# A decoder step on one core: features as rows at both ends, and a norm as one product with a constant matrix

## The chip, the cores and the metric

One core of a Trainium2 chip runs the kernel, in one launch. The metric is the device time of an execution in microseconds (us). TensorE is called PE, VectorE DVE, ScalarE ACT, GpSimd POOL and SyncE SP; ACT, POOL and SP also issue DMAs, POOL those with gathered rows.

## The reference

One layer of a decoder over 256 prompt tokens and 8 x 4 sample tokens, 288 columns in all, with 2048 features, all in fp32:

```
h = h + 1/2 * SwiGLU(RMSNorm(h))                      ffn1: 2048 -> 5632 -> 2048
z = RMSNorm(h) @ w_in                                 3 x 1024 conv, 3 x 1024 q k v, 8 gate logits
h = h + [RMSNorm(conv) | RMSNorm(attention)] @ w_out
h = h + 1/2 * SwiGLU(RMSNorm(h))                      ffn2
h = h + sigmoid(RMSNorm(h) @ w_ple_gate) * (p @ w_ple_proj)
y = RMSNorm(h)
```

RMSNorm(x) is x * rsqrt(mean(x * x) + 1e-6) * gain. The sample tokens attend to 1024 past keys each: `cache_k` holds 80 pages of 128 rows (8 heads x 128 features), and `page_table` names 8 pages for each of the 8 sequences, so 64 pages of 512 KB are read. Besides y, the outputs are the new k, v, forget logits and last conv inputs.

## The kernel before

The residual lies in SBUF with features as rows, `h[128, 16, 288]` (16 tiles of 128 features, 288 tokens as columns). A weight product is made of three: weights and activations are split into a high and a low part (`whi` on ACT, line 257; `wlo` on DVE, line 258; `xh`, `xl`, lines 200 and 201), and lines 290 to 292 add hi*hi, hi*lo and lo*hi in one PSUM bank. `pair()` makes 256 output columns, in chunks of four feature tiles: 24 products of 288 columns, 3.2 us on PE. `run_steps()` goes through a list `steps` of chunks in program order; `load_upto()` issues weight loads eight ahead on SP (line 234), `split_upto()` splits five half-chunks ahead, and `defer(fn, n)` puts a piece of work n chunks later, run by `run_deferred()` in the middle of a chunk. Within one engine instructions run in order; a scheduler fixes that order when the program is built.

The stages follow each other: ffn1, the mixer (gate logits, q, k, conv, v), `w_out`, ffn2, the per-layer embedding (`ple_pair`), `finish`.

**Norms.** `squares()` adds the squared tiles into `acc[128, 288]`. `inv_rms()` (lines 168 to 181) takes three products with a column of 1/2048 that sum over the partitions, tokens as rows, then square root (ACT), reciprocal and a Newton step (DVE) on `[128, 3]`. `spread()` (lines 191 to 197), deferred, brings the 288 factors back to all partitions: three products of a diagonal with ones, and a copy to `rs`. The products run on without waiting, since `rs` is first applied to their results (line 352 and the like). There are seven norms; the one in `finish` needs no spread, since y is there with tokens as rows.

**Key cache.** `k_turn()` (lines 444 to 453) runs between the steps of ffn1, once for each of 64 pages: a gather `kg` on POOL (line 441), 32 x 32 transpositions on DVE (line 450), four DMAs on POOL to a scratch `KD` in HBM (line 452). In the mixer, 32 units `k_scores(n)`, two pages each, read `KT` (1 MB, three buffers), which SP loads from `KD` (line 239); each unit is 16 products (line 704, `KSTEP` sets one every 1.5 chunks).

**Outputs.** `natural()` (lines 623 to 629) transposes three blocks on PE and copies them on DVE, to write tokens as rows: for 8 key heads (`k_out`), 8 value heads and 16 y tiles (`yt`, line 1070 on). `conv_out` (line 882 on) transposes eight tiles, and lines 567 and 569 the forget logits.

**Ends.** Line 466 runs a square root on a `[128, 1]` tile at the start, which brings an ACT table load there. Line 1062 does the same while the last pair runs.

Of the kernel before, what the change touches and what calls it, by code (L numbers as in the profile page):

```python
# [25 lines left out]
P = 128  # L26
# [3 lines left out]
DB = 8  # L30
# [19 lines left out]
TSTEP = 16  # L50
# [8 lines left out]
def constants():  # L59
# [15 lines left out]
    put("ones", np.ones((P, NT)))  # L75
    put("meancol", np.full((P, 1), 1.0 / D))
# [16 lines left out]
def build(nc, tc, ctx, A, O):  # L93
# [69 lines left out]
    ones = const("ones")  # L163
    diag = cst.tile([P, NT], F32, name="diag")
    n0, n1, n2 = (cst.tile([P, 3], F32, name=f"n{i}") for i in range(3))
    v.memset(n0, 1.0)

    def inv_rms(squares, width):

        m = ktbank()  # L170
        for j in range(2):
            pe.matmul(m[:, j:j + 1], squares[:, j * P:j * P + P], const("meancol"), start=True, stop=True)
        pe.matmul(m[:NS, 2:3], squares[:, SEQ:], const("meancol"), start=True, stop=True)
        v.tensor_scalar(n0[:, 0:2], m[:, 0:2], float(D // width), EPS, ALU.mult, ALU.add)
        v.tensor_scalar(n0[:NS, 2:3], m[:NS, 2:3], float(D // width), EPS, ALU.mult, ALU.add)
        s.activation(n1, n0, AF.Sqrt)
        v.reciprocal(n2, n1)
        v.scalar_tensor_tensor(n1, n2, -0.5, n0, ALU.mult, ALU.mult)
        v.tensor_tensor(n1, n1, n2, ALU.mult)
        v.scalar_tensor_tensor(n2, n1, 1.5, n2, ALU.add, ALU.mult)  # L180
        return n2

    def norm_scale(out, squares, width, chunks, more=2):

        def sums():
            r = inv_rms(squares, width)
            defer(lambda: spread(out, r), more)

        defer(sums, chunks)

    def spread(out, r):
# [37 lines left out]
    def load_upto(n):  # L229
        while state["loaded"] < min(n, len(items)):  # L230
# [180 lines left out]
    def first(c):  # L411
        run = steps[2 + c][1]

        def fn():
# [13 lines left out]
            if c == 7:  # L428
                norm_scale(rs, acc, D, 2, 1)
# [5 lines left out]
    KD = drp.tile([DB * PAGES // 2, P, 2, 4, NH * 32], F32, name="KD")  # L435

    KG = {}

    def k_fetch(j):
        KG[j] = W["kg"][0].tile([P, NH * P], F32, name="kg", tag="kg", bufs=4)  # L440
        g.indirect_dma_start(out=KG[j], out_offset=None, in_=A["cache_k"],  # L441
                             in_offset=bass.IndirectOffsetOnAxis(ap=idx[:, j:j + 1], axis=0))

    def k_turn(j):

        for i in range(3) if j == 0 else (j + 2,):
            if i < DB * PAGES:
                k_fetch(i)
        t = W["kg"][0].tile([P, 4, NH, 32], F32, name="kt", tag="kt", bufs=3)
        v.transpose(t, KG.pop(j).rearrange("p (h d c) -> p d h c", d=4, c=32))  # L450
        for i in range(4):
            g.dma_start(KD[j // 2, :, j % 2, i].rearrange("(d c) n -> c d n", c=32),  # L452
# [703 lines left out]
```

## Time and profile before

| | us |
|---|---|
| median of 3 runs | 2376.87 |
| the runs | 2375.11, 2376.87, 2378.67 |
| the profiled execution | 2380.13 |
| its span in the trace | 2378.2 |

| engine | busy us | share of the span | instructions |
|---|---|---|---|
| PE | 2350.4 | 99% | 17792 |
| DVE | 1426.0 | 60% | 2575 |
| ACT | 1052.7 | 44% | 1858 |
| POOL | 495.6 | 21% | 681 |

Products on PE are pipelined: one of 288 columns is listed with some 0.29 us, but its successor starts 0.133 us later at full clock. So the time that an instruction takes from PE is read from the starts of its neighbours, not from its duration.

### The profile page before, as it was taken

The page shows a single profiled execution, that of the slowest core. Times are in us where ns is not written, and L with a number is a line of the kernel's source. Part 1 is how long each engine was busy: PE and PEld are TensorE (multiplying, and loading weights), DVE is VectorE, ACT ScalarE, POOL GpSimd, SP SyncE. Part 2 cuts the span into 40 slices and gives each one's busy share as a digit, 9 for nine tenths or more (in the row PEclk, how much of TensorE's full clock was granted, in tenths as well). Part 3 has the DMA queues.
Part 4 walks back from the last instruction along what each step waited for, and adds up shares of the span by engine and source line. Part 5 has one row for each costly group of instructions (what it writes and reads, how often), then busy time and mean ns, then how long its engine had stood idle before and what let it go on. Part 6 is the DMA issues. An engine that isn't in the chain of part 4 may idle for free.

```text
span 2378.2 us, 45847 instructions
## 1 busy us (share of the span) xinstructions
PE 2350.4 (99%) x17792; PEld 2284.3 (96%) x17792; DVE 1426.0 (60%) x2575; ACT 1052.7 (44%) x1858; POOL 495.6 (21%) x681
## 2 busy tenths in 40 slices
PE   8999999999999999999999999999999999999997
PEld 8999999999999999888788999999999999999997
DVE  6567666666655675456456775555555555555765
ACT  6434444444444553243234454444444444444654
POOL 1044443543400121113446210000000000000110
PEclk9999999999999999999999999999999999999998
DMA  8589898898865566997887654545555555555552
GB/s 263 160 266 316 275 299 289 294 321 270 285 213 161 167 170 218 312 305 234 305 274 271 214 166 150 182 149 180 165 164 168 162 167 163 165 165 164 160 160 80
DMA packets 408601, 510.81 MB, mean 215 GB/s; under 512 B 22064, under 2 KB 376592, under 8 KB 404256
## 3 DMA queue, kind: packets, MB, share of 16 engines
q1 hardware_dynamic: 374560, 401.45, 54.1%
q0 software_dynamic: 33632, 106.13, 12.9%
q8 instruction: 139, 2.28, 0.4%
q14 instruction: 78, 0.64, 0.1%
q10 hardware_dynamic: 192, 0.32, 0.1%
HBM read 469.19 MB, written 38.63 MB: 214 GB/s over the span
## 4 chain that ended last, share of the span: by engine, by line
PE 94%; DMA 3%; issue 1%; DVE 1%; POOL 1%; ACT 0%; SPq 0%; POOLq 0%; DVEq 0%; ACTq 0%
PE mm L290 30%; PE mm L292 29%; PE mm L291 29%; PE va L704 1%; DMA page<-in_cache_v_dram,idx 1%; PE va L761 1%; PE va L290 1%; PE va L292 1%; PE va L291 1%; DMA kg<-in_cache_k_dram,idx 1%; DMA wraw<-in_w_in_dram 1%; DMA wraw<-in_w_out_dram 0%; DVE wlo L258 0%; POOL page L242 0%; PE kt L196 0%
## 5 line engine op out<-in xcount | busy, mean ns | idle before, releaser
L258 DVE TENSOR_TENSOR wlo<-wraw,whi 128x512 fp32r<-128x512 f32 x1384 | 968.7, 706 | 726.9 <-ACT whi L257 680.4
L257 ACT ACTIVATE whi<-wraw 128x512 fp32r<-128x512 f32 x1384 | 862.6, 630 | 982.4 <-PE mm L291 912.5
L290 PE MATMUL mm<-xh,whi 128*128 128x288 f32 x3680 | 1098.4, 298 | 0.2 <-DVE tg L352 0.2
L292 PE MATMUL mm<-xh,wlo 128*128 128x288 f32 x3680 | 1082.6, 294 | 3.5 <-DVE wlo L258 3.5
L291 PE MATMUL mm<-xl,whi 128*128 128x288 f32 x3680 | 1086.0, 295 | 0.0
L290 PEld LDWEIGHTS mm<-xh,whi 128*128 128x128 f32 x3680 | 690.1, 188 | 22.6 <-ACT whi L257 13.6
L292 PEld LDWEIGHTS mm<-xh,wlo 128*128 128x128 f32 x3680 | 693.2, 188 | 4.2 <-DVE wlo L258 4.2
L291 PEld LDWEIGHTS mm<-xl,whi 128*128 128x128 f32 x3680 | 691.4, 188 | 0.2
L290 PE MATMUL mm<-hh,whi 128*128 128x288 f32 x1408 | 416.8, 296 | 0.0
L291 PE MATMUL mm<-hl,whi 128*128 128x288 f32 x1408 | 415.4, 295 | 0.0
L292 PE MATMUL mm<-hh,wlo 128*128 128x288 f32 x1408 | 414.0, 294 | 0.0
L356 POOL TENSOR_TENSOR sr<-sg,rs 128x288 f32<-128x288 f32 x88 | 73.9, 840 | 1108.1 <-ACT sg L354 1108.0
L292 PEld LDWEIGHTS mm<-hh,wlo 128*128 128x128 f32 x1408 | 265.2, 188 | 0.0
L291 PEld LDWEIGHTS mm<-hl,whi 128*128 128x128 f32 x1408 | 264.4, 188 | 0.0
L290 PEld LDWEIGHTS mm<-hh,whi 128*128 128x128 f32 x1408 | 263.8, 187 | 0.0
L452 POOL DMA_DIRECT2D KD<-kt x256 | 142.4, 562 | 84.0 <-DVE kt L450 58.8
L220 POOL TENSOR_TENSOR acc<-acc,sq 128x288 f32<-128x288 f32 x60 | 50.5, 841 | 270.5 <-ACT sq L219 236.7
L450 DVE STREAM_TRANSPOSE kt<-kg 128x1024 f32<-128x1024 f32 x64 | 79.2, 1238 | 34.1 <-DMA kg<-in_cache_k_dram,idx 26.6
L376 DVE SCALAR_TENSOR_TENSOR h<-mm,h 128x288 f32<-128x288 f32 x192 | 86.9, 455 | 21.2 <-PE mm L292 20.7
L441 POOL DMA_INDIRECT kg<-in_cache_k_dram,idx x64 | 71.8, 1122 | 73.7 <-DVE idx L157 53.4
L363 ACT ACTIVATE hh<-hd 128x288 fp32r<-128x288 f32 x88 | 39.1, 445 | 99.6 <-DVE hd L361 99.4
L354 ACT ACTIVATE sg<-tg 128x288 f32<-128x288 f32 x88 | 39.1, 444 | 97.0 <-DVE tg L352 96.9
(274 smaller groups left out, 1559.0 us busy)
## 6 DMA issues: line engine op xcount, KB each, us to landing
wraw<-in_w_ffn_gate_dram SPq DMA_DIRECT2D x176, 512.0 KB, 3.9
wraw<-in_w_ffn_up_dram SPq DMA_DIRECT2D x176, 512.0 KB, 3.6
wraw<-in_w_ffn_down_dram SPq DMA_DIRECT2D x160, 512.0 KB, 3.7
wraw<-in_w_in_dram SPq DMA_DIRECT2D x96, 512.0 KB, 4.8
KD<-kt POOLq DMA_DIRECT2D x256, 128.0 KB, 5.7
KT<-KD SPq DMA_DIRECT2D x32, 1024.0 KB, 7.4
wraw<-in_w_out_dram SPq DMA_DIRECT2D x32, 512.0 KB, 4.5
wraw<-in_w_ple_gate_dram SPq DMA_DIRECT2D x32, 512.0 KB, 4.2
```

Source lines behind the costliest of these rows:

```text
L220: (v if k >= KT - last_on_v else g).tensor_tensor(acc, acc, sq, ALU.add)
L257: s.activation(hi, x, AF.Copy)
L258: v.tensor_tensor(lo, x, hi.bitcast(F32), ALU.subtract)
L290: pe.matmul(o, hi[:, j % 2, w], xh, start=f, stop=False)
L291: pe.matmul(o, hi[:, j % 2, w], xl, start=False, stop=False)
L292: pe.matmul(o, lo[:, j % 2, w], xh, start=False, stop=l)
L354: s.activation(u, t, AF.Silu)
L356: g.tensor_tensor(r, u, rs, ALU.mult)
L376: v.scalar_tensor_tensor(h[:, k, :], o, 0.5, h[:, k, :], ALU.mult, ALU.add)
L441: g.indirect_dma_start(out=KG[j], out_offset=None, in_=A["cache_k"], in_offset=bass.IndirectOffsetOnAxis(ap=idx[:, j:j + 1], axis=0))
L450: v.transpose(t, KG.pop(j).rearrange("p (h d c) -> p d h c", d=4, c=32))
L452: g.dma_start(KD[j // 2, :, j % 2, i].rearrange("(d c) n -> c d n", c=32), t[32 * i:32 * i + 32].rearrange("c d h r -> c d (h r)"))
```

## The change

**Norms.** `mean` is a 128 x 128 matrix of 1/2048. One fp32 product with it sums over the partitions and has the result on all of them, 288 columns wide; ACT takes the logarithm and exp(-ln/2), DVE makes the Newton step on `[128, 288]` in three operations. `spread`, `diag` and the square root go. The last two tiles' squares are not added in `finish` but are parts of the same product.

**Key cache.** The host hands `cache_k` over with features as rows, (page, feature) by (head, row). `KT` is filled by two gathers on POOL a unit. `k_turn`, `KD`, `kg` and the loads on SP go.

**Outputs.** k, y, the conv inputs and the forget logits are written with features as rows and are turned on the host; v stays. `finish` scales `h` in place with seven DVE and two POOL operations and writes eight pieces, alternately from SP and ACT.

**Ends.** The square root at the start goes. The table for the last norm is loaded while the last pair runs.

```diff
-    ones = const("ones")
-    diag = cst.tile([P, NT], F32, name="diag")
...
+    ones = const("ones").to_broadcast([P, NT])
...
-    def inv_rms(squares, width):
-
-        m = ktbank()
-        for j in range(2):
-            pe.matmul(m[:, j:j + 1], squares[:, j * P:j * P + P], const("meancol"), start=True, stop=True)
-        pe.matmul(m[:NS, 2:3], squares[:, SEQ:], const("meancol"), start=True, stop=True)
...
+    def log_tables():
+        tc.keep_in_program_order(s.preload_act_table_set("natural_log_exp_and_others"))
+
+    def inv_rms(out, parts, width, load=True):
+
         b = ktbank()
-        for j, n in enumerate((P, P, NS)):
-            c = slice(j * P, j * P + n)
-            v.tensor_scalar(diag[:n, c], ident[:n, :n], r[:n, j:j + 1], None, ALU.mult)
-            pe.matmul(b[:, c], ones[:n, :P], diag[:n, c], start=True, stop=True)
-        v.tensor_copy(out, b[:, :NT])
+        m = b[:, :NT]
+        for i, x in enumerate(parts):
+            pe.matmul(m, const("mean"), x, start=i == 0, stop=i == len(parts) - 1)
+        if load:
+            log_tables()
+        c = float(D // width)
+        s.activation(ra, m, AF.Ln, bias=eps, scale=c)
+        s.activation(out, ra, AF.Exp, scale=-0.5)
+        v.scalar_tensor_tensor(ra, out, -0.5 * c, out, ALU.mult, ALU.mult)
+        v.scalar_tensor_tensor(ra, m, EPS / c, ra, ALU.add, ALU.mult)
+        v.scalar_tensor_tensor(out, ra, 1.5, out, ALU.add, ALU.mult)
+
+    def norm_scale(out, squares, width, chunks):
+
+        defer(lambda: inv_rms(out, [squares], width), chunks)
...
-                t = W["kt"][0].tile([P, 2, 4, NH, 32], F32, name="KT", tag="KT", bufs=3)
-                sy.dma_start(t.rearrange("p a i h r -> p (a i h r)"), it["src"])
+                t = W["kt"][0].tile([P, 2, NH, P], F32, name="KT", tag="KT", bufs=3)
+                for i, r in enumerate(it["rows"]):
+                    g.indirect_dma_start(out=t[:, i].rearrange("p h s -> p (h s)"), out_offset=None, in_=it["src"],
+                                         in_offset=bass.IndirectOffsetOnAxis(ap=r, axis=0))
...
-    steps.insert(50 + TSTEP * 13, ([], lambda: (closed("kg"), opened("kt", "right"))))
-    for j in reversed(range(DB * PAGES)):
-        steps.insert(50 + TSTEP * j // 5, ([], lambda j=j: k_turn(j)))
-    steps.insert(46, ([], lambda: opened("kg", "right")))
-
-    warm = cst.tile([P, 1], F32, name="warm")
-    v.memset(warm, 1.0)
-    s.activation(warm, warm, AF.Sqrt)
+    steps.insert(200, ([], lambda: opened("kt", "right")))
...
+        g.dma_start(O["logfT"], lf)
...
-            pe.transpose(np_[:, j * NH:j * NH + NH], lf[:, j * P:j * P + P], ident[:NH, :NH])
...
+                if scale is None:
+                    g.dma_start(O["kT"][hh], t)
...
+            if i8 == CB - 1:
+                g.dma_start(O["convT"], M["uc"])
...
-    for i in range(4):
-        at(4 * i + 4, lambda i=i: defer(lambda: k_out(2 * i)), lambda i=i: defer(lambda: k_out(2 * i + 1), 3))
...
-                tc.keep_in_program_order(s.activation(warm, warm, AF.Sqrt))
+                log_tables()
...
-            c = slice(k * P, k * P + P)
-            defer(lambda: natural(E["yn"][:, :, c], E["ys"][:, c], y), 2)
+                E["sq", k] = w.tile([P, NT], F32, name=f"sq{k}")
+                s.activation(E["sq", k], h[:, k, :], AF.Square)
+            if k < KT - 2:
+                s.activation(h[:, k, :], h[:, k, :], AF.Copy, scale=gain("norm_final", k))
...
+        inv_rms(rs, [acc, E["sq", KT - 2], E["sq", KT - 1]], D, False)
+        for i, e in enumerate((v, g, v, v, v, g, v, v)):
+            c = slice(2 * i, 2 * i + 2)
+            if i == KT // 2 - 1:
+                for k in (KT - 2, KT - 1):
+                    v.scalar_tensor_tensor(h[:, k], h[:, k], gain("norm_final", k), rs, ALU.mult, ALU.mult)
             else:
+                e.tensor_tensor(h[:, c], h[:, c], rs.unsqueeze(1).to_broadcast([P, 2, NT]), ALU.mult)
+            (sy, s)[i % 2].dma_start(O["yT"][:, c], h[:, c])
```

Three places in the order of instructions show what moved. First, ACT at the start of the program (x is loaded to `h`, the gains to `gT`; DMAHW semaphores are those of the loads). Before:

```order
L467 DMA gT<-in_gains_dram 128x120
L466 ACT_TABLE_LOAD
L466 ACTIVATE warm<-warm 128x1 [waits DVE_49]
L200 ACTIVATE xh<-h,gT 128x288 [waits DMAHW1_49,DMAHW0_49]
L200 ACTIVATE xh<-h,gT 128x288
L257 ACTIVATE whi<-wraw 128x512 [waits DMAHW2_49]
```

and of the change:

```order
L433 DMA gT<-in_gains_dram 128x120
L190 ACT_TABLE_LOAD [waits DMAHW1_49]
L190 ACTIVATE xh<-h,gT 128x288 [waits DMAHW0_49]
L190 ACTIVATE xh<-h,gT 128x288
L249 ACTIVATE whi<-wraw 128x512 [waits DMAHW2_49]
```

The table load, which waited for nothing, now waits for the first load of x.

Second, DVE in ffn1 where the key pages begin (`idx` are the page rows, `wlo` the low halves of weights, `tg` an eviction). Before:

```order
L157 TENSOR_SCALAR idx<-ptb,consts 128x64 [waits DMAHW3_49]
L258 TENSOR_TENSOR wlo<-wraw,whi 128x512 [waits PE_49,Activation_49]
L258 TENSOR_TENSOR wlo<-wraw,whi 128x512 [waits DMAHW2_49,PE_49,Activation_49]
L450 STREAM_TRANSPOSE kt<-kg 128x1024 [waits DMASW1_49]
L258 TENSOR_TENSOR wlo<-wraw,whi 128x512 [waits PE_49,Activation_49] x2
L450 STREAM_TRANSPOSE kt<-kg 128x1024 [waits DMASW2_49]
```

and of the change:

```order
L156 TENSOR_SCALAR idx<-ptb,consts 128x64 [waits DMAHW3_49]
L250 TENSOR_TENSOR wlo<-wraw,whi 128x512 [waits PE_49,Activation_49]
L250 TENSOR_TENSOR wlo<-wraw,whi 128x512 [waits DMAHW2_49,PE_49,Activation_49]
L250 TENSOR_TENSOR wlo<-wraw,whi 128x512 [waits PE_49,Activation_49] x3
L250 TENSOR_TENSOR wlo<-wraw,whi 128x512 [waits DMAHW4_49,PE_49,Activation_49]
L344 TENSOR_TENSOR tg<-mm,rs 128x288 [waits PE_49]
```

The weight halves no longer stand behind transpositions that wait for gathers (DMASW). On POOL, the gathers of the first three units stand at this place.

Third, POOL among the key-score units of the change (`tB`, `tC` and `acc_82` belong to the conv group; before, POOL had no key loads here):

```order
L850 TENSOR_TENSOR tB<-tB,cy 128x256 [waits DVE_49]
L853 TENSOR_TENSOR tB<-tB,cy 128x32
L230 DMA KT<-in_cache_k_dram,idx 128x1024 [waits DMASW1_49,DMASW0_49,PE_49]
L850 TENSOR_TENSOR tB<-tB,cy 128x256 [waits DVE_49]
L853 TENSOR_TENSOR tB<-tB,cy 128x32
L230 DMA KT<-in_cache_k_dram,idx 128x1024
L861 TENSOR_TENSOR acc_82<-acc_82,sq 128x288 [waits Activation_49]
L230 DMA KT<-in_cache_k_dram,idx 128x1024 [waits DMASW3_49,DMASW2_49,PE_49]
```

The gathers of a unit wait for PE's products of the unit three before it, and the conv group's additions stand between them.

## Rows read from the trace of the kernel before

**Rows 1.** The profile page: its head, and the first line of its section on the chain of work that ended last (share of the span by engine).

```profile
span 2378.2 us, 45847 instructions
...
PE 94%; DMA 3%; issue 1%; DVE 1%; POOL 1%; ACT 0%; SPq 0%; POOLq 0%; DVEq 0%; ACTq 0%
```

**Rows 2.** The table of stretches, for 1400 to 2250 us. [...]

```profile
1400.00:2250.00 850.00, 850.00 (x6378) 849.78 (x6377) 474.47 (x795) 383.53 (x656) 47.52 (x58) 1.00 0.54 165
```

**Rows 3.** The timeline of PE around the norm ahead of ffn1: the last weight product before and the first after the sums of squares (lines 172 and 173), then the same for the spread (line 196). Columns here and below: start in us, duration in us, engine, line, operation, out<-in, stationary size, tile, count.

```profile
39.30 0.30 PE L292 MATMUL mm<-xh,wlo 128*128 128x288 f32 x1
...
40.02 0.40 PE L290 MATMUL mm<-xh,whi 128*128 128x288 f32 x1
...
43.18 0.29 PE L292 MATMUL mm<-xh,wlo 128*128 128x288 f32 x1
...
44.18 0.40 PE L290 MATMUL mm<-xh,whi 128*128 128x288 f32 x1
```

**Rows 4.** The timeline of PE around the score products of one prompt head (lines 805 and 806, fp32).

```profile
1222.40 0.29 PE L292 MATMUL mm<-xh,wlo 128*128 128x288 f32 x1
1222.53 0.38 PE L805 MATMUL kt<-k,q 128*128 128x128 f32 x2
1222.75 0.60 PE L806 MATMUL kt<-k,q 128*128 128x256 f32 x2
1223.00 0.48 PE L290 MATMUL mm<-xh,whi 128*128 128x288 f32 x1
```

**Rows 5.** The timeline of PE: the weight products on both sides of one key head's three transpositions (lines 625 to 627), and on both sides of the six of two y tiles.

```profile
939.53 0.29 PE L292 MATMUL mm<-xh,wlo 128*128 128x288 f32 x1
...
939.91 0.38 PE L290 MATMUL mm<-xh,whi 128*128 128x288 f32 x1
...
2275.64 0.29 PE L292 MATMUL mm<-xh,wlo 128*128 128x288 f32 x1
...
2276.35 0.38 PE L290 MATMUL mm<-xh,whi 128*128 128x288 f32 x1
```

**Rows 6.** The timelines of DVE and then of PE around the first key transpositions (line 450). In brackets stands the idle time just before an instruction and what ended it.

```profile
130.35 0.26 DVE L157 TENSOR_SCALAR idx<-ptb,consts 128x64 int32<-128x64 int32 x1 [3.04 <-DMA ptb<-in_page_table_dram]
...
136.82 1.25 DVE L450 STREAM_TRANSPOSE kt<-kg 128x1024 f32<-128x1024 f32 x1 [5.02 <-DMA kg<-in_cache_k_dram,idx]
137.99 1.25 DVE L258 TENSOR_TENSOR wlo<-wraw,whi 128x512 fp32r<-128x512 f32 x2
...
152.05 1.25 DVE L450 STREAM_TRANSPOSE kt<-kg 128x1024 f32<-128x1024 f32 x1 [4.09 <-DMA kg<-in_cache_k_dram,idx]
...
136.41 0.29 PE L291 MATMUL mm<-xl,whi 128*128 128x288 f32 x1
138.70 0.40 PE L292 MATMUL mm<-xh,wlo 128*128 128x288 f32 x1 [1.99 <-DVE wlo L258]
...
152.16 0.29 PE L291 MATMUL mm<-xl,whi 128*128 128x288 f32 x1
153.93 0.40 PE L292 MATMUL mm<-xh,wlo 128*128 128x288 f32 x1 [1.47 <-DVE wlo L258]
```

**Rows 7.** The timeline of all engines at the start.

```profile
1.18 1.28 ACT L466 ACT_TABLE_LOAD   x1 [1.18 <-PEq L1139]
...
2.48 0.20 ACT L466 ACTIVATE warm<-warm 128x1 f32<-128x1 f32 x1
...
4.23 0.96 ACT L200 ACTIVATE xh<-h,gT 128x288 fp32r<-128x288 f32 x2 [1.55 <-DMA h<-in_x_dram]
...
5.70 1.15 ACT L257 ACTIVATE whi<-wraw 128x512 fp32r<-128x512 f32 x2 [0.51 <-DMA wraw<-in_w_ffn_gate_dram]
...
6.38 0.61 PE L290 MATMUL va<-xh,whi 128*128 128x288 f32 x1 [6.38 <-ACT whi L257]
```

**Rows 8.** The timeline of all engines after the last weight product, and one row of the table of DMA issues (KB each, median us from issue to landing).

```profile
2361.16 0.29 PE L292 MATMUL mm<-ph,wlo 128*128 128x288 f32 x1
...
2362.28 0.45 DVE L1069 TENSOR_TENSOR h<-h,sg 128x288 f32<-128x288 f32 x1
...
2367.91 0.49 DVE L1094 TENSOR_SCALAR yn<-yn,n 128x512 f32<-128x512 f32 x1
...
2368.82 3.11 SPq L1101 DMA_DIRECT2D out_dram<-yn  x4
...
wraw<-in_w_ffn_down_dram SPq DMA_DIRECT2D x32, 256.0 KB, 3.0
```

**Rows 9.** The timeline, POOL and DVE, during the last stage.

```profile
2304.28 0.81 POOL L220 TENSOR_TENSOR acc<-acc,sq 128x288 f32<-128x288 f32 x1
...
2304.56 1.68 DVE L258 TENSOR_TENSOR wlo<-wraw,whi 128x512 fp32r<-128x512 f32 x2 [1.25 <-ACT whi L257]
```

**Rows 10.** The chain of waits in order of time, with key-score units (start, duration); then from the groups of POOL by line the key gathers' issue (busy us, mean ns of one | idle before), and from the table of DMA issues their median us to landing.

```profile
925.04 1.00 PE va L704 x16
...
941.75 0.98 PE va L704 x13
...
L441 POOL DMA_INDIRECT kg<-in_cache_k_dram,idx x64 | 71.8, 1122 | 73.7 <-DVE idx L157 53.4 <-issue 18.9 <-DMA KD<-kt 1.4
...
kg<-in_cache_k_dram,idx POOLq DMA_INDIRECT x64, 7.0
```

**Rows 11.** The table of PE's waits (us in total, times, longest us).

```profile
PE va L761 <- DMA page<-in_cache_v_dram,idx: 2.5, 5, 1.1
```

More of the change, by code (lines that the diff above doesn't have):

```diff
@@ L74, in constants @@
     put("ident", np.eye(P))
-    put("ones", np.ones((P, NT)))
-    put("meancol", np.full((P, 1), 1.0 / D))
+    put("ones", np.ones((P, 1)))
+    put("mean", np.full((P, P), 1.0 / D))
     put("iota", rows[:, None])
@@ L183, in norm_scale @@
[L183 to L191, printed above, removed]
-        b = ktbank()
-        for j, n in enumerate((P, P, NS)):
-            c = slice(j * P, j * P + n)
-            v.tensor_scalar(diag[:n, c], ident[:n, :n], r[:n, j:j + 1], None, ALU.mult)
-            pe.matmul(b[:, c], ones[:n, :P], diag[:n, c], start=True, stop=True)
-        v.tensor_copy(out, b[:, :NT])
+    ones = const("ones").to_broadcast([P, NT])
@@ new lines, in build @@
+    ra = cst.tile([P, NT], F32, name="ra")
+    eps = cst.tile([P, 1], F32, name="eps")
+    v.memset(eps, EPS)
+    def log_tables():
+        tc.keep_in_program_order(s.preload_act_table_set("natural_log_exp_and_others"))
+    def inv_rms(out, parts, width, load=True):
+        b = ktbank()
+        m = b[:, :NT]
[9 more added lines that the diff above has]
+        v.scalar_tensor_tensor(out, ra, 1.5, out, ALU.add, ALU.mult)
@@ L433, in build @@
         first(c)
[L435 to L450, printed above, removed]
-        for i in range(4):
-            g.dma_start(KD[j // 2, :, j % 2, i].rearrange("(d c) n -> c d n", c=32),
-                        t[32 * i:32 * i + 32].rearrange("c d h r -> c d (h r)"))
+    steps.insert(200, ([], lambda: opened("kt", "right")))
     def later_loads():
@@ L629, in natural @@
         v.tensor_copy(dst_sample, t[:NS, 2 * P:3 * P])
-    def k_out(hh):
-        kp = W["kp"][0]
-        kn, ks = kp.tile([P, 2, P], F32, name="kn", tag="kn"), kp.tile([NS, P], F32, name="kns", tag="kns")
-        natural(kn, ks, k_[hh])
-        c = slice(hh * P, hh * P + P)
-        g.dma_start(O["k_prompt"][:, c].rearrange("(j p) c -> p j c", p=P), kn)
-        g.dma_start(O["k_sample"][:, c], ks)
     def v_evac(i):
@@ L690, in k_scores @@
         seq = 4 * gi + bb
-        it = dict(kind="k", src=KD[seq * PAGES // 2 + pp].rearrange("p a i n -> p (a i n)"))
+        it = dict(kind="k", src=A["cache_k"], rows=[idx[:, j:j + 1] for j in (seq * PAGES + 2 * pp, seq * PAGES + 2 * pp + 1)])
         def fn():
@@ L704, in fn @@
                     pe.matmul(sb[32 * c:32 * c + 32, :2 * P], strip[:, hh, at:at + 32],
-                              it["tile"][:, :, :, hh, :].rearrange("p a i r -> p (a i) r"),
+                              it["tile"][:, :, hh, :],
                               start=first and half == 0, stop=last and half == 1, tile_position=(0, 32 * c))
@@ L927, in kv_start @@
         opened("kq", "right")
-        opened("kp", "right")
         q_gather()
@@ L933, in v_start @@
     def v_start():
-        for n in ("kp", "kq", "kt"):
+        for n in ("kq", "kt"):
             closed(n)
@@ L1048, in ple_start @@
             v.tensor_tensor(E["lo"][:, k, :], pa[:, k, :], E["hi"][:, k, :].bitcast(F32), ALU.subtract)
-        E["yn"] = w.tile([P, 2, D], F32, name="yn")
-        E["ys"] = w.tile([NS, D], F32, name="ys")
     def ple_pair(i):
@@ L1069, in proj @@
             v.tensor_tensor(h[:, k, :], h[:, k, :], sg[b], ALU.add)
-            y = w.tile([P, NT], F32, name="yt", tag="yt", bufs=4)
             if k < KT - 2:
-                s.activation(y, h[:, k, :], AF.Copy, scale=gain("norm_final", k))
                 squares(k, w)
             else:
-                squares(k, w, 1)
-                v.tensor_scalar(y, h[:, k, :], gain("norm_final", k), None, ALU.mult)
-            c = slice(k * P, k * P + P)
-            defer(lambda: natural(E["yn"][:, :, c], E["ys"][:, c], y), 2)
+                E["sq", k] = w.tile([P, NT], F32, name=f"sq{k}")
+                s.activation(E["sq", k], h[:, k, :], AF.Square)
+            if k < KT - 2:
+                s.activation(h[:, k, :], h[:, k, :], AF.Copy, scale=gain("norm_final", k))
         return (pair(A["w_ple_gate"], i * 256, ks, xact, gate, **(dict(late=1, tag="va") if i == 0 else {}))
@@ L1149 @@
         A[name] = nc.dram_tensor(f"in_{name}_dram", a.shape, _mybir.dt.from_np(a.dtype), kind="ExternalInput").ap()
-    for i, (name, shape, _) in enumerate(_OUTS):
+    for i, (name, shape) in enumerate(_OUTS):
         O[name] = nc.dram_tensor(f"out_{i}_dram", shape, F32, kind="ExternalOutput").ap()
@@ L1154 @@
     r = _run(nc, [arrays], core_ids=[0])
-    return tuple(r.results[0][f"out_{i}_dram"].reshape(shape) for i, (_, _, shape) in enumerate(_OUTS))
+    return results(*(r.results[0][f"out_{i}_dram"].reshape(shape) for i, (_, shape) in enumerate(_OUTS)))
```

67 lines of the change are left out of this document (18 added, 49 removed).

## The prediction

> **What bounds the kernel now.** I first read the page's head and its chain of waits [rows 1]: the span is 2378.2 us and 94% of the chain that ended last is TensorE (PE), so time goes only if PE work goes or a PE stall goes. The profiled execution took 2380.13 us, 3.3 above the median of the three runs (2376.87); I make the sum against the profiled one and carry the difference over. Next, the table of stretches [rows 2]: between 1400 and 2250 us PE is busy for all 850 us with 6378 products, one every 0.133 us, while VectorE (DVE) works 474 us of them, ScalarE (ACT) 384, and the DMA engines stand at 0.54. So an instruction taken from PE's queue moves all that is behind it; no other engine has to catch up first. The price of such an instruction is therefore not its duration but its **block**: the start of the next weight product, less the start of the last one before it, less 0.133.
>
> **Norms, on PE.** A norm now stops the weight products twice. Its sums take 40.02 − 39.30 − 0.13 = 0.59, its spread (three products with a diagonal) 44.18 − 43.18 − 0.13 = 0.87 [rows 3]. Six of the seven norms lie inside the stream (the last stands in the tail): 6 × 1.46 = 8.8. In their place comes one fp32 product over 288 columns. The trace has none; the nearest is the pair of fp32 products of a prompt head, 128 and 256 columns, whose block is 1223.00 − 1222.40 − 0.13 = 0.47 [rows 4]. By columns 288/384 × 0.47 = 0.35 is the low end; the spread's 0.87, also 288 fp32 columns but with three weight loads, is the high end. I take 0.40, near the head's row because it too has few weight loads: 2.4. Norms: **−6.4** (−3.6 to −6.7). The new chain behind the product (logarithm, exponential, three DVE operations 128x288, a table load) takes some 4 us of ACT and DVE. The scale is first read in a deferred eviction more than a chunk (3.2 us of PE) behind, where the old spread came two chunks after its sums, and ACT and DVE have about half of the stretch free [rows 2]; so I cost it at nothing. Without that cover an eviction late by more than a bank's time would cost PE some 2 us a norm.
>
> **Outputs, on PE.** The three transpositions of a key head block 939.91 − 939.53 − 0.13 = 0.25; the six of two y tiles 2276.35 − 2275.64 − 0.13 = 0.58 [rows 5]. Eight heads: −2.0. Sixteen y tiles are eight such pairs, one of them in the tail: 7 × 0.58 = −4.1. Eight conv transpositions and two of the forget logits at up to 0.10 each (0.58 / 6): −0.7. **Together −6.8.** The copies on DVE and the output DMAs they fed hid beside PE and give nothing; the new output DMAs (one for a key head, one for all of conv) are fewer.
>
> **Stalls at the key transpositions.** DVE runs in order, and its first transpositions wait for gathers: DVE is idle 5.02 us before 136.82 and 4.09 before 152.05, with weight halves queued behind. PE pays: no product starts between 136.41 and 138.70, nor between 152.16 and 153.93 [rows 6]; less 0.13 each, 2.16 + 1.64 = 3.8. In the changed program DVE has no key transposition. The wait for the index just ahead (3.04 us idle before 130.35) stays, and no stall of PE followed it: five halves split ahead cover some 3 us. **−3.8** (0 to −4.2; zero if the six key gathers that now start there make something else late).
>
> **The head.** Now the ACT table load starts at 1.18 and takes 1.28, the warm-up operation follows at 2.48, and the first split of x starts at 4.23 when x has landed; weights land and are split at 5.70, and the first product starts at 6.38 [rows 7]. In the changed order the load stands behind the wait for x. So: load 4.2 to 5.5, two splits of x (0.96) to 6.45, weights 6.45, first product 7.1: **+0.8** (0.7, the step of the first product just worked out, to 1.3, the whole load). The row gives the load as 1.28 with the next operation right behind it (2.48 − 1.18 = 1.30). [...]
>
> **The tail.** The last product starts at 2361.16, scaling starts at 2367.91, the first output DMA at 2368.82, and the engines move the 2.4 MB of the result to the end [rows 8]. Changed: the last residual tile, now ready at 2362.73, needs no scaling ahead of it any more (ready at 2362.5) and its square no additions; square 0.5, one product of three parts 0.5, Ln and Exp 0.5 each, three DVE operations 0.45 each, by the like rows [rows 7, 8], make 3.4 and, with some 0.1 at each hand-over, scaling starts at about 2366.4, 1.5 earlier. But then seven operations on DVE and two on POOL scale the 16 tiles, and the two engines exclude each other: POOL's addition at 2304.28 ends at 2305.09, and the two DVE operations begun at 2304.56 took 1.68 [rows 9], where two alone take 1.25 [rows 6]. One after the other: five double tiles on DVE at about 0.7 (512 columns take 0.63), POOL's two at 1.6 (twice 0.81), two single ones at 0.45 make 7.6 us. The last of the eight pieces (295 KB) leaves at 2374.0 and lands some 3.1 later (256 KB of weights take 3.0 [rows 8]): 2377.1. **−1.0** (0, if POOL's pair is dearer by 1 us, to −2, if half of POOL's time is beside DVE's).
>
> **The key loads.** They move from SyncE (SP), 1 MB each, to two indirect gathers each on GpSimd (POOL), released by PE's use of the unit three before. On PE a unit of 16 products starts at 925.04 and the third one after it at 941.75 [rows 10]; the first is through with its tile 1.0 later, which leaves 15.7 us, 15.2 without the key transpositions between (every other unit has a chunk more). A gather's issue takes 1.12, and it lands in 7.0 [rows 10]: 2 × 1.12 + 7.0 = 9.3 of 15.2. The spare 5.9 us hold POOL's additions of about 0.9 each that the new order puts between. **0**, with the price of the opposite in the rivals. Bytes in that stretch are the same.
>
> **Page loads of the values** stall PE now for 2.5 us in waits [rows 11] and keep their order on POOL behind fewer output DMAs; 0, give or take 2.
>
> **Sum:** −6.4 − 6.8 − 3.8 + 0.8 − 1.0 = −17.2. 2380.1 − 17.2 = 2362.9 for a profiled run; at the median 2376.9 − 17.2 = **2359.7 us**.
>
> **Rivals.**
> (a) Less gain: a norm product at 0.87 (+2.8), stalls at 130 to 160 us only moved (+3.8), a tail that gains nothing (+1.0). All three give 2367.3. For it: the six gathers start exactly where DVE waits for the index now. Against: nothing on DVE or PE needs them before 915 us.
> (b) More gain: the waits for value pages go too (−2.5), the lower ends of the norm and the tail (−1.3): 2355.9.
> (c) **Slower: the key gathers come late.** Mechanism: POOL runs in order, and behind a gather that waits for PE stand the additions that DVE waits for; ahead of it may stand one that waits for DVE. Each of some 15 short-spaced units would then hold PE. It decides when issue and landing take more than 15.2 us from the release; beyond that each us costs 15. To be 4.8 us slower than before (21.9 above the sum's result) each must be 1.5 late, 16.7 us instead of 9.3; at 1.6 late the time is 2359.7 + 24 = 2384. Against it speaks the issue of 1.12, a mean over 64 gathers that ran beside DVE's splits and transpositions [rows 10]. [...]
> (d) No effect: PE's extra work was hidden after all and the same time returns as waits for weights. The fully busy 850 us speak against it; the time would be 2377.
>
> **Chances.** A measurement of this kernel tells a change from none from about 0.2%, 4.8 us, on: faster is under 2372.1, slower over 2381.6. My sum with (a) and (b) around it 0.91, (d) 0.05, (c) 0.04. The sum's result is the likeliest single time: (a) 0.14, (b) 0.12, 0.65 between. The range reaches from below (b), for a shorter run of value waits than I can price, to (a): 2354 to 2368.
>
> **What would show it.** Right: one product of 288 columns a norm with a block near 0.40; no product from the ends of key, y and conv blocks; no gap over 0.5 us at 136 and 152; the first product at about 7.1; key units 4.3 and 7.6 us apart with no wait for a gather; an end some 16 us after the last weight product. Wrong: PE waiting at the key products for a DMA, waits for weights in the 1400 to 2250 stretch, or a norm that PE or DVE waits for.

## The result and the profile after

The changed kernel takes **2354.32 us** (median of 4 runs, 2352.13 to 2361.34); the kernel before, on the same chip, 2377.77 (2375.11 to 2379.31). The ratio is 0.9901, 95% interval 0.9890 to 0.9913: 23.5 us less, where 17.2 were forecast. The turning of `cache_k` and of the outputs, which the host now does, is not in this time. The profiled execution took 2361.34, the slowest of its four, with a span of 2359.4: against the profiled one of before, 18.8 less.

The page's head and the shares of the chain that ended last, to be read against [rows 1]:

```profile
span 2359.4 us, 44872 instructions
...
PE 96%; DMA 2%; DVE 1%; issue 1%; ACT 0%; POOL 0%; DVEq 0%; POOLq 0%; ACTq 0%
```

PE has 96% of the chain now. The table of stretches for 130 to 160 us, for the rest of ffn1 and for ffn2. Its columns, here and in [rows 2]: start and end, length, busy us of PE, of PE's weight loads, of DVE, ACT and POOL (with their instructions), granted PE clock (1.00 is full speed), share of the DMA engines, GB/s.

```profile
130.00:160.00 30.00, 30.00 (x227) 30.00 (x227) 16.47 (x27) 12.93 (x22) 8.30 (x8) 1.00 0.80 280
200.00:860.00 660.00, 660.00 (x4952) 660.00 (x4952) 370.37 (x613) 298.03 (x512) 37.52 (x46) 1.00 0.52 166
1400.00:2230.00 830.00, 830.00 (x6228) 830.00 (x6227) 461.36 (x762) 372.21 (x637) 45.77 (x57) 1.00 0.52 165
```

In the first row PE is busy for all 30 us: the gaps of [rows 6] are gone. In the other two it is busy throughout, as in [rows 2], so nothing has taken PE's place as the bound. The norm ahead of ffn1 in the timeline of PE, which answers to [rows 3]:

```profile
40.70 0.29 PE L284 MATMUL mm<-xh,wlo 128*128 128x288 f32 x1
40.84 0.65 PE L175 MATMUL kt<-acc,consts 128*128 128x288 f32 x2
41.10 0.51 PE L282 MATMUL mm<-xh,whi 128*128 128x288 f32 x1
41.45 0.29 PE L283 MATMUL mm<-xl,whi 128*128 128x288 f32 x1
```

The product with the constant matrix is listed as two instructions, and its block is 41.10 − 40.70 − 0.13 = **0.27**. But the weight product behind it is followed only 0.35 later, so another 0.21 is lost there. Around [rows 3] that second loss is 0.10 each time.

The head, in the timeline of all engines, against [rows 7]:

```profile
4.51 1.28 ACT L190 ACT_TABLE_LOAD   x1 [4.51 <-DMA h<-in_x_dram]
...
5.81 0.96 ACT L190 ACTIVATE xh<-h,gT 128x288 fp32r<-128x288 f32 x2
...
6.67 0.61 ACT L249 ACTIVATE whi<-wraw 128x512 fp32r<-128x512 f32 x1
...
7.34 0.61 PE L282 MATMUL va<-xh,whi 128*128 128x288 f32 x1 [7.34 <-ACT whi L249]
```

The table load waits for x, lasts 1.28 and is followed at once (4.51 + 1.28 = 5.79; the split starts at 5.81). The first product starts at 7.34 in place of 6.38.

The tail, against [rows 8]:

```profile
2343.91 0.29 PE L284 MATMUL mm<-ph,wlo 128*128 128x288 f32 x1
...
2345.39 0.30 PEld L175 LDWEIGHTS kt<-sq,consts 128*128 128x128 f32 x2 [1.16 <-ACT sq L1018]
...
2349.15 5.84 DVE L1037 TENSOR_TENSOR h<-h,rs 128x576 f32<-128x576 f32 x5
2349.20 3.84 POOL L1037 TENSOR_TENSOR h<-h,rs 128x576 f32<-128x576 f32 x2 [15.77 <-DVE rs L183]
2349.93 5.45 SPq L1038 DMA_DIRECT2D out_dram<-h  x4
...
2354.91 0.94 DVE L1035 SCALAR_TENSOR_TENSOR h<-h,gT,rs 128x288 f32<-128x288 f32 x2
```

From the last weight product to the end of the span it is 2359.4 − 2343.9 = 15.5 us in place of 17.0. Five DVE operations take 5.84 us and two of POOL's 3.84, at the same time. Two of the five are listed with 1.95 each, those beside POOL's; the other three with 0.75. So DVE takes longer while POOL works, as in [rows 9].

The key units in the chain of waits, against [rows 10]:

```profile
919.29 1.00 PE va L662 x16
...
935.67 1.00 PE va L662 x16
```

Their gathers' issue among POOL's groups by line (busy us, mean ns | idle before):

```profile
L230 POOL DMA_INDIRECT KT<-in_cache_k_dram,idx x64 | 62.8, 981 | 130.6 <-PE va L662 64.4 <-DVE idx L156 54.0 <-issue 11.6
```

and their landing in the table of DMA issues:

```profile
KT<-in_cache_k_dram,idx POOLq DMA_INDIRECT x64, 5.9
```

From the first unit (919.29) to the last (1104.04) they come 4.39 and 7.60 us apart, with one exception of 8.16, where other products stand between; PE waits for no key gather. Issue (0.98) and landing (5.9) are a little shorter than before.

PE's waits for value pages, against [rows 11]:

```profile
PE va L719 <- DMA page<-in_cache_v_dram,idx: 6.2, 4, 2.7
```

and one of them in the timeline of PE:

```profile
1162.59 1.06 PE L719 MATMUL va<-page,PT 128*32 128x512 f32 x6
1166.34 2.56 PE L719 MATMUL va<-page,PT 128*32 128x512 f32 x10 [2.69 <-DMA page<-in_cache_v_dram,idx]
1168.82 0.61 PE L282 MATMUL mm<-xh,whi 128*128 128x288 f32 x1
```

Here PE waits 2.7 us for a page, and the next weight product is listed with 0.61 us, like the first of the program [rows 7]. The granted clock there, in the table of stretches:

```profile
1167.50:1170.90 3.40, 3.40 (x11) 2.08 (x10) 0.42 (x1) 0.00 (x0) 2.54 (x3) 0.50 0.72 202
1170.90:1174.30 3.40, 3.40 (x27) 3.40 (x27) 1.24 (x2) 1.27 (x2) 0.39 (x1) 1.00 1.06 373
```

From 1.1 us behind the wait on, the granted clock is 0.50 for 3.4 us, and weight products start 0.24 apart in place of 0.133; then it is 1.00 again. The same follows a wait of 2.6 us that ends at 1258.5. An estimated 1.7 us go with each of the two, half of 3.4. This execution lost 6.2 us to listed page waits and has two such pieces, the one of before 2.5 and one piece. The unprofiled executions have no trace, but this is the likely reason why the two profiles differ by less than the medians.

**The ledger.** Of all starts of PE's products I took 0.133 for each weight product and gave the rest to what stands between. It is for the same pair of profiles. One norm and part of the conv transpositions lie inside the stretch of the value pages; they stand in their own lines (some 1.6 us), and the last line is the stretch without them:

| term | forecast | found |
|---|---|---|
| norms in the stream | −6.4 | −7.1 (block 0.27, not 0.40) |
| key, y, conv and logit transpositions | −6.8 | −6.7 |
| slow weight products right behind those blocks, less those behind the new norms | none | −1.7 |
| stalls at the key transpositions | −3.8 | −4.7 (a third gap of 0.3, 0.6 of slow products) |
| head | +0.8 | +1.0, and 0.4 of products 0.24 apart |
| tail | −1.0 | −1.5 |
| key loads | 0 | 0 |
| sum | −17.2 | −20.3 |
| stretch of the value pages | 0 ± 2 | +1.5 in this pair, about −3 on average (below) |

### The profile page after: what moved, and what is told of

Its sections match the earlier page's. It is cut to its first block, busy times and chain, and to the rows that moved or that the text cites. A ratio compares the mean times of both kernels' runs of the same rounds, so it can differ in the third digit from the quotient of the medians.

```text
span 2359.4 us, 44872 instructions
## 1 busy us (share of the span) xinstructions
PE 2332.4 (99%) x17650; PEld 2269.8 (96%) x17650; DVE 1342.3 (57%) x2407; ACT 1055.1 (45%) x1857; POOL 338.4 (14%) x410
## 4 chain that ended last, share of the span: by engine, by line
PE 96%; DMA 2%; DVE 1%; issue 1%; ACT 0%; POOL 0%; DVEq 0%; POOLq 0%; ACTq 0%
PE mm L282 30%; PE mm L284 30%; PE mm L283 30%; PE va L662 1%; DMA page<-in_cache_v_dram,idx 1%; PE va L719 1%; PE va L282 1%; PE va L284 1%; PE va L283 1%; DMA wraw<-in_w_in_dram 0%; PE kt L282 0%; PE kt L283 0%; PE kt L284 0%; PE kt L175 0%; DVE h L1037 0%
## 5 line engine op out<-in xcount | busy, mean ns | idle before, releaser
L230 POOL DMA_INDIRECT KT<-in_cache_k_dram,idx x64 | 62.8, 981 | 130.6 <-PE va L662 64.4
L234 POOL DMA_INDIRECT page<-in_cache_v_dram,idx x64 | 68.3, 1067 | 51.4 <-DVE wlo L250 37.4
L356 DVE TENSOR_TENSOR hl<-hd,hh 128x288 fp32r<-128x288 f32 x88 | 40.8, 464 | 22.0 <-ACT hh L355 22.0
```

What stands on the lines that cost most here:

```text
L230: g.indirect_dma_start(out=t[:, i].rearrange("p h s -> p (h s)"), out_offset=None, in_=it["src"], in_offset=bass.IndirectOffsetOnAxis(ap=r ...
L356: v.tensor_tensor(H["lo"][:, k, :], t, H["hi"][:, k, :].bitcast(F32), ALU.subtract)
```

## The experiments

Times are medians of four to six runs (ten for before2). Ratios go against the kernel before, measured beside them; its own medians there lie between 2378.54 and 2379.79, so that a difference of 1 us between two experiments says little. "Stretch" is the time from the first value-page product to the last, in the profile: 193.9 us before, 194.0 in the first profile of the change. Each diff is against the changed kernel.

**1. again**: the changed kernel, unaltered.

> The changed kernel once more, unaltered. Theory (PE's queue sets the time, what was taken off it adds up to about 18 us, and the value-page waits vary from run to run): 2352 to 2361 us, 22 to 24 below the kernel before at the median; outside 1100 to 1330 us the profile's blocks and gaps equal those of the first profile within 0.5 us in sum, and a profiled time t goes with value-page waits of about 6.2 - (2361.3 - t) us. Rival (the part beyond the forecast comes from norms or key loads and is there in each run): the page waits are again about 6 us, whatever the time.

2355.44 us (2353.85 to 2358.02), 0.9905 (0.9891 to 0.9920); profiled at 2355.78, span 2353.7, 5.7 below the first profile. PE's waits between 1100 and 1330 us in it:

```profile
PE va L719 <- DMA page<-in_cache_v_dram,idx: 2.7, 3, 1.5
PE kt L744 <- DVE so L738: 1.0, 1, 1.0
```

The stretch as a row of the table of stretches, in the first profile:

```profile
1118.90:1312.90 194.00, 187.78 (x1357) 154.27 (x1356) 104.52 (x241) 72.32 (x150) 96.12 (x112) 0.98 0.83 284
```

and in this one:

```profile
1118.10:1307.20 189.10, 185.29 (x1358) 152.99 (x1356) 105.06 (x241) 71.95 (x150) 95.92 (x112) 1.00 0.86 292
```

The stretch is 189.0 long, 5.0 shorter, and the granted clock 1.00 in place of 0.98. All else agrees within 0.8. So the same program differs by 5 us there, and a profiled time must not be read without looking at that stretch. The waits differ by 2.5 us (6.2 against 2.7 and 1.0), and the two pieces at a granted clock of 0.50 are gone, an estimated 3.4: together somewhat more than the 5.0. The expectation held for the time and for what varies, but its formula gave 0.7 us of page waits where 2.7 were found: the clock and the wait for a DVE result were not in it.

**2. before2**: the kernel before, unaltered.

> The kernel before, unaltered, for a second profile. Theory (the value-page waits vary from run to run, there too): the stretch from the first value-page product to the last differs from the first profile's 193.9 us by up to 5, and the time goes with it; all else is equal within 0.5 us. Rival (the stretch is fixed before the change and varies only after it): 193.9 again.

2379.94 us (2375.84 to 2381.91), 0.9999 (0.9990 to 1.0009). The stretch is 196.8, 2.9 longer than in the first profile, the tail 0.9 shorter and the stalls at the key transpositions 1.7 shorter (2.4 in place of 4.1). So the stretch varies there too, as expected, but "all else equal within 0.5" was too narrow. Of these stretches about 1.6 us are norm and conv products that the change removes; like for like before has 192.3 and 195.2. Seven profiles of the change with that part of the program unaltered give 187.8 to 194.0, mean 190.3. The difference, about 3.4, is most of what the ledger leaves open to the medians, 23.5 against 20.3, but rests on two profiles against seven. The listed page waits do not explain it: 2.5 and 4.1 us before, 1.4 to 6.2 in the seven, 3.2 in the mean. Pieces at a granted clock of 0.50 give an estimated 1.0 of it, at 1.7 each: one in each of the two, three in all seven.

**3. norm_old**: norms inside the stream as before.

```diff
-        defer(lambda: inv_rms(out, [squares], width), chunks)
+        def sums():
+            r = inv_rms3(squares, width)
+            defer(lambda: spread(out, r), more)
+
+        defer(sums, chunks)
```

> The changed kernel with the six norms inside the stream made as before (sums with tokens as rows, square root, spread by a diagonal); the last norm stays as changed. Theory (blocks on PE): 7 us more, all of it at the norms' places. Rival (the new chain of logarithm, exponential and three wide DVE operations costs PE something that the forecast left at nothing): less than 5 more. Rival (the part of the gain beyond the forecast is the norms'): 10 or more.

0.9948 (0.9935 to 0.9961). Five runs lie between 2362.35 and 2366.66 with 2366.05 in the middle, 10.6 above again; a sixth, of 7317 us, is left aside. The profile, taken at 2362.35, is 6.8 above that of again: the blocks are back, as the timeline of PE shows,

```profile
40.03 0.50 PE L195 MATMUL kt<-consts,acc 128*128 128x1 f32 x4
40.46 0.22 PE L196 MATMUL kt<-consts,acc 128*32 128x1 f32 x2
...
43.92 0.94 PE L219 MATMUL kt<-diag,consts 128*128 128x128 f32 x6
```

and the ledger gives 7.0 at the norms' places. The profile bears out the theory; the median goes with the rival of "10 or more". The profiled run is the fastest of the five, so what the others lost is not in any trace. I count 7 as shown and the rest as open.

**4. key_old**: the key path as before (gathers, transpositions, scratch, loads on SP).

```diff
+    for j in reversed(range(DB * PAGES)):
+        steps.insert(50 + TSTEP * j // 5, ([], lambda j=j: k_turn(j)))
...
+                sy.dma_start(t.rearrange("p a i h r -> p (a i h r)"), it["src"])
```

> The changed kernel with the key path as before: gathers, DVE transpositions, scratch in HBM, loads on SP. Theory (only the two stalls at 136 and 152 us): 4 us more, both gaps on PE there again. Rival (the old key path also held up weight or value loads, which explains the gain beyond the forecast): 8 to 10 more, with longer waits for value pages between 1100 and 1330 us. Rival (the new gathers on POOL cost PE something): under 2 more.

2362.11 us (2360.25 to 2365.65), 6.7 above again; 0.9934 (0.9921 to 0.9947). The gaps on PE are back, though smaller than in [rows 6]; the timeline of PE:

```profile
137.10 0.40 PE L283 MATMUL mm<-xh,wlo 128*128 128x288 f32 x1 [0.97 <-DVE wlo L249]
...
151.04 0.40 PE L283 MATMUL mm<-xh,wlo 128*128 128x288 f32 x1 [0.20 <-DVE wlo L249]
```

The ledger gives 2.5 for them (with slow products), 2.2 for a longer stretch (191.2), and 3.9 for a tail of 19.4: the last output packet ends at 2357.2, as early after the last product as elsewhere, but the final barrier is reached only at 2362.2. What the barrier waited for is not in the trace. So the theory's 4 is confirmed in kind, in size between 2.5 and 4.7 over three profiles (slow products included); the rest of the 6.7 is open. PE waited 4.8 us for value pages here, 2.7 in again, which is the direction of the first rival but within what the same program scatters (2.7 and 6.2).

**5. out_old**: the transpositions of 8 key heads and 14 y tiles put back.

```diff
+        at(4 * i + 4, lambda i=i: defer(lambda: k_out(2 * i)), lambda i=i: defer(lambda: k_out(2 * i + 1), 3))
...
+                defer(lambda: natural(E["yn"][:, :, c], E["ys"][:, c], h[:, k, :]), 2)
```

> The changed kernel with the transpositions of eight key heads and of the first 14 y tiles put back on PE and DVE, as before; their results go nowhere (no output DMA from them), the outputs are written as in the change. Theory (blocks on PE): eight of 0.25 and seven of 0.58, 6 us more, at those places and nowhere else, apart from the value-page waits, which vary by some 5 us from run to run. Rival (they hid beside other waits of PE): under 2 more. Rival (their DVE copies also hold up something): over 8.

2363.29 us (2361.22 to 2364.17), 7.9 above again, 7.1 if each is taken against the kernel before beside it; 0.9931 (0.9917 to 0.9944). The profile is 7.7 above again's: 6.0 in the blocks, as expected, and most of the rest in the weight products right behind them, each followed about 0.1 late (1.2 outside the stretch). That part is the term that the forecast's definition of a block left out.

**6. conv_old**: conv transpositions and their eight small DMAs on POOL put back.

```diff
+            defer(lambda: conv_out(b, uc), 2)
...
+                g.dma_start(CN[0:2, c], u["n"][0:2, :])
+                g.dma_start(CN[2:18, c], u["n"][2:18, :])
```

> The changed kernel with the eight conv transpositions on PE and their eight small output DMAs on POOL put back (to a scratch in HBM, beside the new output). Theory A (they only take PE's time): 0.5 to 1 us more, the stretch of the value pages at 188 to 191 us in the profile. Theory B (their DMAs stood ahead of page gathers on POOL and waited for DVE, and so cost the kernel before the extra 4 us between its value-page stretch and that of the change): 3 to 5 more, the stretch at 192 to 196 us.

2355.56 us (2354.32 to 2355.68), 0.9901 (0.9886 to 0.9916); stretch 187.3, the shortest of all. Theory B falls: these DMAs alone do not make the stretch longer. Of A's 0.5 to 1 us only 0.1 shows in the time, within its scatter.

**7. warm**: a warm-up operation at the start.

```diff
+    warm = cst.tile([P, 1], F32, name="warm")
+    v.memset(warm, 1.0)
+    s.activation(warm, warm, AF.Copy)
     s.dma_start(gT, A["gains"])
```

> The changed kernel with a warm-up operation of one column at the start again, so that the table load waits for nothing. Theory (load of 1.28 us on the path of the head): first product at 6.4 in place of 7.34, 1.0 us less in all. [...] Rival 2 (the weights' landing sets the head anyway): no change.

2356.31 us (2355.31 to 2356.97), 0.9907 (0.9893 to 0.9921): no gain in the time. The head in the timeline of ACT and PE:

```profile
1.19 1.28 ACT L435 ACT_TABLE_LOAD   x1 [1.19 <-PEq L1087]
2.48 0.20 ACT L435 ACTIVATE warm<-warm 128x1 f32<-128x1 f32 x1
4.80 0.96 ACT L190 ACTIVATE xh<-h,gT 128x288 fp32r<-128x288 f32 x2 [2.11 <-DMA gT<-in_gains_dram]
6.12 1.15 ACT L249 ACTIVATE whi<-wraw 128x512 fp32r<-128x512 f32 x2 [0.36 <-DMA wraw<-in_w_ffn_gate_dram]
...
6.80 0.61 PE L282 MATMUL va<-xh,whi 128*128 128x288 f32 x1 [6.80 <-ACT whi L249]
```

The table load is hidden again, but x and the gains landed at 4.80 here, so the first product starts at 6.80, 0.5 below the change. Over the profiles the first product comes at 6.4 to 6.8 with a warm-up (four) and at 6.9 to 7.5 without (ten): 0.7 between the means. So the load takes its 1.28, but on the way to the first product it is worth about half of that: with it hidden, ACT waits for the weights (0.36 here), which is a part of rival 2. The theory's 1.0 less does not show. In the first profile of the change, the next ACT operation starts 0.01 to 0.28 us after the end of each of its eleven table loads, the longest where it waits for PE.

**8. kt2**: two buffers for the key tiles.

```diff
-                t = W["kt"][0].tile([P, 2, NH, P], F32, name="KT", tag="KT", bufs=3)
+                t = W["kt"][0].tile([P, 2, NH, P], F32, name="KT", tag="KT", bufs=2)
```

> The changed kernel with two KT buffers in place of three: a unit's gathers are released by the unit two before, which leaves 4.4 + 7.6 - 1.1 = 10.9 us each time in place of 15 or 18. Theory (issue 0.98 twice, landing 5.9 median: some 8 us): no wait of PE, or single ones under 1 us; time within 3 us of the change. [...]

2354.96 us (2354.54 to 2360.29), 0.9906 (0.9891 to 0.9921). The units in the chain of waits keep their spacing:

```profile
918.77 1.00 PE va L662 x16
923.17 1.00 PE va L662 x16
930.76 1.00 PE va L662 x16
935.15 1.00 PE va L662 x16
```

With 10.9 us in place of 15 no unit waits, so the forecast's slower case would have needed gathers over 4 us later than they come. In the first profile of the change the issue of these gathers takes 0.98 in the mean, with DVE busy for 95 of the 190 us from 915 to 1105.

**9. tail_v**: all scaling at the end on DVE.

```diff
-        for i, e in enumerate((v, g, v, v, v, g, v, v)):
+        for i, e in enumerate((v,) * 8):
```

> The changed kernel with all tiles of the end scaled on DVE, POOL's two operations moved there. Theory (DVE and POOL exclude each other, so POOL's two of 1.9 us only add): seven of about 0.75 and two of 0.45 in 6.2 us in place of 6.7; the tail 0.5 to 1 us shorter than 15.5. Rival (POOL works beside DVE): the tail 1 us or more longer.

2356.78 us (2356.36 to 2357.41), 0.9906 (0.9891 to 0.9921); in the timeline:

```profile
2345.49 4.77 DVE L1037 TENSOR_TENSOR h<-h,rs 128x576 f32<-128x576 f32 x7
2346.27 4.38 SPq L1038 DMA_DIRECT2D out_dram<-h  x4
...
2350.17 0.94 DVE L1035 SCALAR_TENSOR_TENSOR h<-h,gT,rs 128x288 f32<-128x288 f32 x2
```

Seven operations now take 4.77 us, where five beside POOL took 5.84: POOL's two cost DVE more time (an estimated 2.4 us, 5.84 less five of 0.68) than DVE needs to do them itself (1.4). The tail is 14.7, 0.8 shorter. The time does not show it; the stretch was 190.5 here and 189.0 in again.

**10. vstep28** and **11. vstep286**: the value rounds further apart.

```diff
-VSTEP = 2.7
+VSTEP = 2.8
```

> The changed kernel with the value rounds every 2.8 chunks in place of 2.7: three rounds in place of five have only two weight chunks ahead of them. Theory (a page is asked for eight loads ahead; before a round with two chunks that is some 6 to 8 us, less than four issues of 1.07 and a landing of 6.3): waits at two rounds fewer, 2 to 3 us less. Rival (the DMA engines' rate sets the stretch, whatever the spacing): within 1 us.

> As the run before with 2.86 chunks, and the attention norm one chunk later (two-chunk gaps at rounds 1, 8 and 15 only). Theory: like 2.8, 2 to 3 us below the change. Rival (the last round now ends so late that the norm or the second half of w_out waits for it): a new gap of 1 to 3 us on PE behind the last round, no gain or a loss.

2356.08 (2354.53 to 2357.54), 0.9902 (0.9887 to 0.9917), and 2359.88 us (2358.17 to 2362.21), 0.9921 (0.9907 to 0.9934). With 2.8 PE waits for a page only once, 2.3 us, and yet nothing is gained; with 2.86 it waits elsewhere too (up to 1.8 us at a time for ACT and DVE results behind the rounds). The theory of the two-chunk rounds names the places of 6.0 of the 6.2 us in the first profile (rounds 4, 11 and 14, counted from 0), but in again 1.5 of 2.7 us fall on round 12, which has three chunks ahead of it. Fewer such rounds did not make the kernel shorter.

**12. best**: warm-up, scaling on DVE, and nine buffers for weights and pages in place of eight.

```diff
-RAW = 8
+RAW = 9
...
-    idx = cst.tile([P, 64], I32, name="idx")
+    idx = ptb
...
+        ra = parts[0]
```

> The changed kernel with three things more: the warm-up operation at the start, all of the end's scaling on DVE, and nine buffers for weights and value pages in place of eight (room for it comes from the norm's scratch tile, for which the squares' own tile is used, and from the page index, which is made in place). Theory (a page waits because it is asked for only eight loads ahead): each page comes one load, 2 us or more, earlier, the stretch from the first value-page product to the last goes from some 189 us to 185 or less; with 0.5 from the head and 0.8 from the tail 4 to 6 us below the change, about 2350. Rival (the DMA engines' rate sets that stretch): it stays at 187 to 191, and only 1.3 us is gained, about 2354.

2356.91 us (2354.70 to 2357.50), 0.9902 (0.9885 to 0.9918). The first product starts at 6.43 and the tail is 14.8, as hoped. PE's longest waits:

```profile
PE kt L594 <- DVE vt L604: 7.4, 2, 6.4
PE va L282 <- ACT whi L249: 6.4, 1, 6.4
```

The stretch (192.3 us) in the table of stretches:

```profile
1117.50:1309.80 192.30, 182.71 (x1354) 153.32 (x1356) 105.91 (x241) 71.33 (x150) 95.27 (x111) 0.98 0.86 287
```

The longest of the waits inside the stretch, in the timelines of ACT, DVE and PE:

```profile
1196.43 1.15 ACT L249 ACTIVATE whi<-wraw 128x512 fp32r<-128x512 f32 x2 [7.48 <-DMA wraw<-in_w_in_dram]
...
1197.10 1.29 DVE L250 TENSOR_TENSOR wlo<-wraw,whi 128x512 fp32r<-128x512 f32 x2 [6.97 <-ACT whi L249]
1198.31 0.45 DVE L604 TENSOR_TENSOR vt<-mm,rs 128x288 f32<-128x288 f32 x1
...
1198.81 0.48 PE L594 MATMUL kt<-consts,vt 128*128 128x128 f32 x1 [6.40 <-DVE vt L604]
```

No product waits for a page any more. Instead a value tile's transposition waits 6.4 us for DVE, DVE for a weight half of ACT's, and ACT 7.48 us for a weight load. The wait has moved from the pages to the weights. What SP, which issues that load, had waited for just before (1175 to 1192 us; in total, times, longest):

```profile
SPq L224 <- PE va L722: 10.1, 1, 10.1
SPq L224 <- DVE wlo L250: 2.0, 1, 2.0
```

Weights and pages share the nine buffers, and the loads go out at 1189.8 to 1190.8, when PE's page products and DVE's split have freed them. The theory fails, as far as one profile shows: the pages no longer hold PE, but the stretch did not shrink. The rival gave 187 to 191 and about 2354, and neither came out. That the rate of the DMA engines sets the stretch is not shown either. It moves the same 55 MB (189.1 us at 292 GB/s, 194.0 at 284, 192.3 at 287), but this rate is only the bytes over the length, and it reaches 295 in conv_old. The DMA engines' share is 0.86 here, and in pieces of 4 us it runs from 0.23 to 1.07. So the loads come in bursts, and what would bring them earlier is open. No version here beats the changed kernel by more than the runs scatter.

## Why the prediction was right

The measured 2354.32 lies 0.3 us above the low end of the range of 2354 to 2368, and 5.4 below the sum's 2359.7. The mechanism held: the ledger's terms add to −20.3 where the forecast had −17.2. That the time still fell inside the range is partly luck, since some 3 us more came from the value pages, which the forecast put at 0.

**What bounds the kernel.** Right: PE is the bound before and after, and what is taken from its queue comes off the end. Each of the three large parts that were put back cost its blocks or gaps again (7.0 for the norms, 2.5 for the stalls, 6.0 and 1.2 for the outputs, by the ledgers). Their medians rose by more for the norms and the key path (10.6 and 6.7), and that excess is open.

**Norms.** Right in kind, more than forecast: the block is 0.27, below the low end of 0.35 that was scaled from the prompt heads' products, so the term is −7.1, outside its −3.6 to −6.7. The 0.21 lost behind the new product equals the two times 0.10 behind the old ones, so it does not change the term. The chain behind the product cost PE nothing, as forecast: no product waits for it in the table of PE's waits.

**Outputs.** Blocks right (6.7 against 6.8). The step that failed is the definition of a block: its end was put at the start of the next weight product, but that product itself runs longer and its successor starts about 0.1 late. Over the blocks that went, less the new ones, that is 1.7 us.

**Stalls.** Right in kind and place, and in this pair a little beyond the range's 4.2 (4.1 in gaps and 0.6 of slow products). A second profile of before has 2.4, so this term has a spread of its own that a single trace does not show.

**Head and tail.** Right in sign; +1.0 for +0.8, and 0.4 more from products that start 0.24 apart (up to 13.77 us in place of 11.84), where the granted clock reads 1.00; −1.5 for −1.0. Both vary: the first 200 products are through 1.4 us later in this pair but 0.6 later in the mean of the 14 profiles, and the tail before was 17.0 and 16.1 in its two profiles, 15.5 in nearly all without a change there. That DVE takes longer beside POOL (1.95 an operation) was shown by taking POOL's part away: 0.68 an operation, and a tail 0.8 shorter.

**Key loads.** Right; rival (c), late gathers, did not show even with the shorter lead of two buffers.

**Value pages.** Here lies about half of the difference between 17.2 and 23.5; the ledger's 20.3 is the other. The forecast took 0, give or take 2, from one trace. The stretch differs by 5.0 us between two profiles of the same program, and its mean went down by some 3. Which part of the change did that was looked for with the norms, the key path, the outputs and the conv outputs put back one at a time, and is open: none of them alone brought the longer stretch back. Rival (b) named the place, and its 2355.9 is near the measured time, but its mechanism is not what the traces show: the waits for value pages did not go (2.5 and 4.1 us before, 3.2 in the mean of seven after).

## What to carry to other kernels

Where one engine is busy all the time, price an instruction on it by the starts of its neighbours, and take the neighbour behind it into the price too. Before reading a profiled time against another, find the stretch that varies between executions of the same program and take it out of both. And where two kinds of loads share a ring of buffers, removing the wait for one kind can bring a wait for the other, as it did here (page waits gone, 6.4 us at a weight load): look at what released the loads before adding a buffer.

## What the runs showed of the hardware

A fp32 product of 128 x 128 by 288 columns delayed the next weight product by 0.27 us and the one behind that by 0.21. Two POOL operations of 128x576 took 1.92 us each beside DVE's, and DVE's two beside them 1.95, where the same operation on DVE alone took 0.68 (7 in 4.77, tail_v). With a table load at the head of ACT, the operation behind it began 0.02 us after its end. In the first profile of the change the granted clock fell to 0.50 for 3.4 us behind each of two waits of PE of 2.7 and 2.6 us, and in again, where PE waited at most 1.5 at a time in that stretch, its mean over the stretch was 1.00. Length alone does not tell: in the profile of before it fell behind a wait of 1.07 that ended at 1212.71, and stayed at 1.00 behind one of 1.99 that ended at 138.70. At the head of the program, too, weight products start 0.24 apart (up to 13.77 us in the first profile of the change), but there the granted clock reads 1.00.
